# The MLP's first 512 channels by plain products in token halves, and GpSimd's sums moved to VectorE

## The chip, the cores and the metric

The kernel runs on one core of one Trainium2 chip. The metric is the device time of one execution in microseconds (us). Names of engines in the profile: PE is TensorE (PEld its weight loads), DVE is VectorE, ACT is ScalarE, POOL is GpSimd, SP is SyncE, whose queue issues the DMAs.

## The reference

One decoder block on 512 tokens of 1024 channels, float32, with two token mixers (a gated MLP over positions and a state-space scan) whose sum goes through an output projection, and then a channel MLP with 4096 hidden channels. The change is in the MLP:

```python
x = x + merged @ w_out
h2 = rms_norm(x, norm_mlp_g)
x = x + jnp.square(jax.nn.relu(h2 @ w_mlp_up)) @ w_mlp_down
return rms_norm(x, norm_final_g)
```

## The kernel before

Every float32 operand of a product is split into a high part (a ScalarE cast to the matmul's reduced float32 type) and a low part (a VectorE subtraction, "remainder" below), and every product is three matmuls: high by low, low by high, high by high (`mm3`, `trio`). Weights come in slabs of 128 x 1024, 512 KB each, on SP's queue; `parts_of` (L114 to L120) makes the pair `whi`, `wlo`, of which there are four buffers each. `Slabs.take` hands out the next pair and makes further ones ahead of time.

**The up-projection by seven products.** The 4096 hidden channels are eight blocks `u` of 512. For each block the transposed, normalised activations `h2` are four quadrants `b11`, `b12`, `b21`, `b22` (first index: half of the 1024 input channels; second: half of the 512 tokens), and the block's weights are four slabs. Instead of eight products of quadrants the kernel makes seven (the Strassen-Winograd form): it forms sums of weight slabs (`Up.sum`, L860 to L870) and sums of quadrants (`h2_sums`, L792), and seven products `(u, k)`, each of 8 trios, that is 24 matmuls of 256 columns (L155). The operand pairs made from `h2` are `hq[1]` to `hq[7]`. The products' results are put together with copies `kept` (L935), additions (L957), and `act` (L938 to L946: relu, square, cast on ScalarE, remainder on VectorE), which writes `aTs`, the down-projection's input.

**Order.** `items` (L886) is the order of the products and of the down-projection's slabs ("d"); four rounds `qd`, each of two blocks `u` and eight down slabs. In the first round, both blocks' products are interleaved (L883). The section is under a manual schedule: each engine keeps the order in which the program is written, so an instruction that waits holds up all that stands behind it on its engine.

**The start of the MLP.** The second half of the output projection runs token tile by token tile (`tok_major`, order "tokens"). After each of four tiles of 128 tokens `n2_evac` adds the residual, squares (ScalarE, with the sum), takes the power -1/2 (`rms_scale`, on GpSimd), applies the norm's gain (`gain`, two VectorE instructions of 128 x 512, L817), and `h2_tile` transposes the tile on TensorE and copies it into `h2` (L800, L801). `Weave` (`wv.at(delay, f)`) sets after how many matmul groups each step is issued; the delays are `H2D`. Tiles 0 and 1 are the first token half, tiles 2 and 3 the second. The first products use only the first token half (`hq[1]` is -b11, `hq[2]` is b21); tile 2 and tile 3 are transposed between these products. Then `h2_second` makes `hq[3]` and `hq[5]`, and three more quadrant sums follow ahead of products 3, 4 and 5 of the order (`H2AT`), two of them on GpSimd:

```python
h2_sums = (lambda: nc.vector.tensor_add(b12, b12, b22), lambda: nc.gpsimd.tensor_sub(b11, b11, b12),
           lambda: nc.gpsimd.tensor_sub(b21, b21, b12))
```

GpSimd also makes the remainder of `hq[3]` (L772) and one weight sum of block 0 (L870).

Of the kernel before, what the change touches and what calls it, by code (L numbers as in the profile page):

```python
# [11 lines left out]
F32 = mybir.dt.float32  # L12
F32R = mybir.dt.float32r
AF = mybir.ActivationFunctionType
ALU = mybir.AluOpType
# [3 lines left out]
P = 128  # L19
T = 512  # L20
# [11 lines left out]

SD, SA, SI, SS, SB, SC = 9, (12, 20), 8, 7, 9, 9


H2D = 0, 1.5, 2.5, 5.5, .4, 2.2, .6, 6, 7.9, 7.9
H2AT, NR = (3, 4, 5), 6
HPAD = 16, 32, 32, 32, 32, 32, 32, 48
WARM = 2, 0

# [10 lines left out]
def block_kernel(ctx: ExitStack, tc: tile.TileContext, x, w_v, w_all, w_up, wspt, pvec, hvec, g_mix, g_mlp, g_fin, v_g, v_b,  # L51
# [17 lines left out]
    def sm_tile():  # L69
        return ps.tile([P, T], F32, tag="sm", name="sm", bufs=4)  # L70


    class Slabs:
# [24 lines left out]
        def make(self):  # L98
            if self.todo:
                self.ready.append(self.todo.popleft()())  # L100
# [10 lines left out]
            self.ahead(ahead)  # L111
            return s

    def parts_of(raw):  # L114
        n = raw.shape[-1]
        hi = wpool.tile([P, SL], F32R, tag="whi", name="whi", bufs=4)[:, :n]
        lo = wpool.tile([P, SL], F32R, tag="wlo", name="wlo", bufs=4)[:, :n]
        nc.scalar.copy(hi, raw)  # L118
        nc.vector.tensor_sub(lo, raw, hi.bitcast(F32))  # L119
        return hi, lo  # L120
# [5 lines left out]
    class Weave:  # L126
# [3 lines left out]
        def at(self, delay, fn):  # L130
            heapq.heappush(self.due, (self.now + delay, self.seq, fn))
            self.seq += 1
# [25 lines left out]
    def cut(pair, *idx):  # L158
        return tuple(a[(slice(None),) + idx] for a in pair)

    def wk(w, k, n=P):
        return cut(w, slice(k * n, (k + 1) * n))
# [599 lines left out]
    n2.tile([P, HPAD[7]], F32, name="hq_pad8")  # L762
    b11, b12, b21, b22 = (h2[:, 4 * j:4 * j + 4, 256 * l:256 * l + 256] for j in range(2) for l in range(2))

    def hi_of(k, a, scale=1.0):
        if scale == 1.0:
            nc.scalar.copy(hq[k][0], a)
        else:
            nc.scalar.activation(hq[k][0], a, AF.Copy, scale=scale)

    def lo_of(k, a):
        (nc.gpsimd if k == 3 else nc.vector).tensor_sub(hq[k][1], a, hq[k][0].bitcast(F32))  # L772

    def h2_one():
        hi_of(1, b11, -1.0)
        nc.vector.scalar_tensor_tensor(hq[1][1], b11, -1.0, hq[1][0].bitcast(F32), ALU.mult, ALU.subtract)

    def h2_two():
        hi_of(2, b21)
        lo_of(2, b21)  # L780

    h2_first = h2_one, h2_two

    def h2_second():
        nc.vector.tensor_sub(b12, b11, b12)
        hi_of(3, b22)
        hi_of(5, b12)
        lo_of(3, b22)
        lo_of(5, b12)


    h2_sums = (lambda: nc.vector.tensor_add(b12, b12, b22), lambda: nc.gpsimd.tensor_sub(b11, b11, b12),  # L792
               lambda: nc.gpsimd.tensor_sub(b21, b21, b12))
    h2_ops = ((6, b12), (7, b11), (4, b21))

    def h2_tile(h, t):
        for b in range(2):
# [7 lines left out]
    def n2_evac(t, acc):  # L805
        res_evac(1)(t, acc)
        xt, h = x1[:, t, :], nr.tile([P, DM], F32, tag="rms_h", name="rms_h", bufs=1)
        ss = small.tile([P, 1], F32, tag="rms_ss", name="rms_ss", bufs=4)
        rs = []

        def square():
            nc.scalar.activation(hq[4][0].rearrange("p k t -> p (k t)"), xt, AF.Square, accum_out=ss)

        def gain():
            for b in range(2):
                hb = slice(b * T, (b + 1) * T)
                nc.vector.scalar_tensor_tensor(h[:, hb], xt[:, hb], rs[0], gbc[:, hb], ALU.mult, ALU.mult)  # L817

        def scale():
            rs.append(rms_scale(ss))  # L820

        steps[t] = square, scale, gain, lambda: h2_tile(h, t)
        for i in range(3 if t < 2 else 0):
            wv.at(H2D[i], steps[t][i])
        if t < 2:
            wv.at(H2D[3], steps[t][3])
        elif t == 2:
            wv.at(H2D[4], h2_one)
            wv.at(H2D[5], square)
        else:  # L830

            h2_two()
            square()
            for f in (steps[2][1], steps[2][2], scale):
                f()
            for d, f in zip(H2D[6:], (gain, steps[2][3], steps[3][3], h2_second)):
                wv.at(d, f)


# [3 lines left out]
    class Up:  # L843

        def __init__(self):
            self.free, self.n, self.at = list(tiles), 0, {}

            self.todo = [(u, i) for u in range(2 * NQ) for i in (2, 3, None, 0, 1)]
            j = self.todo.index((1, 2))
            self.todo[j:j + 5] = [(1, 0), (1, 1), (1, 2), (1, 3), (1, None)]  # L850

        def pump(self):
            while self.free and self.todo:
# [6 lines left out]
        def sum(self, u, n):  # L860
            self.pump()
            at = lambda i: self.at[u, i]
            if n == 1:
                nc.vector.tensor_add(at(None), at(2), at(3))  # L864
            elif n == 2:
                nc.vector.tensor_add(at(0), at(None), at(0))
            elif n == 3:
                nc.vector.tensor_add(at(2), at(2), at(0))
            else:
                (nc.vector if u else nc.gpsimd).tensor_add(at(1), at(0), at(1))  # L870

        def make(self, u, k):
            self.pump()
            i = {1: 0, 2: 1, 5: None, 6: 0, 3: 1, 7: 2, 4: 3}[k]
            r = parts_of(self.at[u, i])
            if k > 2:
                self.free.append(self.at.pop((u, i)))
                self.pump()
            return r

    up = Up()
    later = [(0, 1), (0, 2), (0, 5), (0, 6), (0, 3), (0, 7), (1, 1), (0, 4), (1, 2), (1, 5), (1, 6), (1, 3), (1, 7)]
    orders = [[(0, 1), (0, 2), (1, 1), (1, 2), (0, 5), (0, 6), (0, 3), (0, 7), (1, 5), (0, 4), (1, 6), (1, 3), (1, 7)]]  # L883
    orders += [later] * (NQ - 1)

    items = []  # L886
    for qd in range(NQ):
        items += [("p", 2 * qd + u, k) for u, k in orders[qd]] + [("d", qd, 0), ("p", 2 * qd + 1, 4)] + [("d", qd, i) for i in range(1, 8)]
    place = {it: j for j, it in enumerate(items)}

    sums_at = collections.defaultdict(list)
    for u in range(2, 2 * NQ):
        j = place["p", u, 5]
        for n, d in ((1, 7), (3, 6), (2, 4), (4, 2)) if u % 2 else ((1, 7), (3, 6), (2, 4), (4, 3)):
            sums_at[j - d].append((u, n))
    sums_at[1].append((0, 4))
    j = place["p", 1, 5]
    for n, d in ((1, 5), (3, 4), (2, 3), (4, 1)):
        sums_at[j - d].append((1, n))
    for it in items:  # L900
        slabs.todo.append(slabs.slab if it[0] == "d" else lambda it=it: up.make(*it[1:]))

    slabs.early = True
# [3 lines left out]
    def n2_evac_(t, acc):  # L907
        n2_evac(t, acc)
        if t == 0:
            up.sum(0, 1)  # L910
            up.sum(0, 3)
        if t == 1:
            up.sum(0, 2)

    up.pump()
    tok_major(mg_t, n2_evac_, order="tokens", ahead=3)
    slabs.ahead(3)
    mg_cm.__exit__(None, None, None)
    mp = ctx.enter_context(pool("mlp"))
    tiles.append(mp.tile([P, SL], F32, name="ut7"))  # L920
# [2 lines left out]
    nc.sync.dma_start(gfb, g_fin.partition_broadcast(P))  # L923
    banks = [acc_tile() for _ in range(4)]
    bank_a, bank_c, bank_d = (banks[0], banks[3]), banks[1], banks[2]
    kept = {}
    aTs = {}
    after, last = collections.defaultdict(list), collections.defaultdict(list)
# [9 lines left out]
    def act(j, u, i, l, src):  # L938

        r_ = mp.tile([P, 2, 256], F32, tag="relu", name="relu", bufs=2)  # L940
        nc.scalar.activation(r_, src.rearrange("p (c t) -> p c t", c=2), AF.Relu)
        nc.scalar.activation(r_, r_, AF.Square)
        n = 4 * (u % 2) + 2 * i
        hi, lo = cut(aTs[u // 2], slice(n, n + 2), slice(256 * l, 256 * l + 256))
        nc.scalar.copy(hi, r_)
        last[j + 1].append(lambda: nc.vector.tensor_sub(lo, r_, hi.bitcast(F32)))  # L946

    def evac(j, u, k, bank, i=0, l=0):

        if k in (1, 5, 6):  # L950
            keep(u, k, bank)
        elif k == 4:
            after[j].append(lambda: act(j, u, 1, 0, bank))
        else:
            k0, i, l = {2: (1, 0, 0), 3: (6, 0, 1), 7: (5, 1, 1)}[k]
            t = kept.pop((u, k0))
            nc.vector.tensor_sub(t, bank, t)  # L957

            jj = NR if j < NR else j
            after[jj].append(lambda: act(jj, u, i, l, t))  # L960

    sums = [[] for _ in range(NT)]

# [22 lines left out]
                nc.sync.dma_start(out[t * P:(t + 1) * P, c], o[:, c])  # L986
        return evac

    BANK = {2: lambda u: bank_c, 5: lambda u: bank_d, 3: lambda u: bank_d}
    accs = {}  # L990
    for j, it in enumerate(items[:-4]):

        if j and items[j - 1][0] == "p":
            _, u, k = items[j - 1]
            evac(j, u, k, BANK.get(k, lambda u: bank_a[u % 2])(u))
        if j == NR:
            nr_cm.__exit__(None, None, None)
            ap = ctx.enter_context(pool("act"))
            new_act(0)
        late = H2AT.index(j) if j in H2AT else None  # L1000
        if late is not None:
            h2_sums[late]()
        for u, n in sums_at.pop(j, ()):
            up.sum(u, n)
        for f in last.pop(j, ()):
            f()
        w = slabs.take(3)
        if late is not None:
            hi_of(*h2_ops[late])
        for f in after.pop(j, ()):  # L1010
            f()
        if late is not None:
            lo_of(*h2_ops[late])
        if it[0] == "p":
            _, u, k = it
            if k == 1 and u % 2 == 0 and u:
# [95 lines left out]
```

## Time and profile before

| | before |
|---|---|
| median of 3 runs | 1074.12 us (1073.47 to 1074.26) |
| the profiled execution's own time | 1073.14 us |
| its span, first to last instruction | 1071.4 us |
| TensorE busy | 1049.6 us, 98% |
| VectorE busy | 682.2 us, 64% |
| ScalarE busy | 505.6 us, 47% |
| GpSimd busy | 150.8 us, 14% |
| mean granted TensorE clock | 0.994 |

The times are the device's; the span leaves out what lies before the first and after the last instruction, 1.7 us here. Busy shares are means over the whole kernel, whose stages have different limits. Matmul records overlap, since a matmul is shown from its start to the end of its passage through the array; the pace is read from the distance of two starts.

### The profile page before, as it was taken

Reading aid. Unit: us, or ns where it says so; the run is one execution under the profiler, and the core shown is the slowest. Engines: PE = TensorE matmul, PEld = TensorE weight load, DVE = VectorE, ACT = ScalarE, POOL = GpSimd, SP = SyncE. Lnnn points to the kernel's source line nnn. Section 1 sums busy time; section 2 is a strip of 40 time slices with the busy share of each in tenths; the row PEclk is TensorE's granted clock in tenths of the full one; section 3 lists DMA queues with packets and bytes.
Section 4 is the critical chain, followed back from the end, with each engine's and each line's share of the span. In section 5 each row is a group of like instructions: output and inputs, shape, how many; then the busy total and the mean of one; then the engine's idle time right before and its main releaser. Section 6 shows DMA issues by size and latency. Waiting matters only on the chain. (4 is left out here: it accounts for less than half of the span.)

```text
span 1071.4 us, 14498 instructions
## 1 busy us (share of the span) xinstructions
PE 1049.6 (98%) x5685; PEld 910.2 (85%) x5685; DVE 682.2 (64%) x1087; ACT 505.6 (47%) x753; POOL 150.8 (14%) x192
## 2 busy tenths in 40 slices
PE   8999999999999999999999999996999999999997
PEld 7988888888888888888888888886989989988986
DVE  5572444446887995657778865369746746745743
ACT  4743333334546547444465532254824733723742
POOL 3020000001432342300324300014000000000000
PEclk9999999999999999999999999998999999999999
DMA  6433224232333233332323233721432432331032
GB/s 204 143 118 118 79 80 138 97 99 79 99 98 118 99 99 102 100 101 96 107 86 99 72 125 98 272 63 59 139 98 79 137 100 79 118 104 55 21 99 79
DMA packets 34630, 111.39 MB, mean 104 GB/s; under 512 B 3969, under 2 KB 4737, under 8 KB 34562
## 3 DMA queue, kind: packets, MB, share of 16 engines
q1 hardware_dynamic: 34560, 110.46, 32.5%
q8 instruction: 45, 0.74, 0.3%
q14 instruction: 23, 0.19, 0.0%
q10 hardware_dynamic: 2, 0.00, 0.0%
HBM read 108.29 MB, written 2.16 MB: 103 GB/s over the span
## 5 line engine op out<-in xcount | busy, mean ns | idle before, releaser
L119 DVE TENSOR_TENSOR wlo<-wraw,whi 128x1024 fp32r<-128x1024 f32 (+1 forms) x146 | 175.5, 1203 | 119.5 <-ACT whi L118 119.5
L118 ACT CAST whi<-wraw 128x1024 fp32r<-128x1024 f32 (+1 forms) x146 | 149.9, 1028 | 165.0 <-PE acc L149 75.9
L147 PE MATMUL acc<-hTl,whi 128*128 128x512 f32 x448 | 179.8, 401 | 0.0
L149 PE MATMUL acc<-hTh,whi 128*128 128x512 f32 x448 | 174.8, 390 | 0.0
L148 PE MATMUL acc<-hTh,wlo 128*128 128x512 f32 x448 | 174.6, 390 | 0.0
L119 DVE TENSOR_TENSOR wlo<-ut,whi 128x1024 fp32r<-128x1024 f32 x56 | 70.5, 1261 | 54.3 <-ACT whi L118 54.2
L149 PEld LDWEIGHTS acc<-hTh,whi 128*128 128x128 f32 x448 | 84.1, 188 | 18.1
L148 PEld LDWEIGHTS acc<-hTh,wlo 128*128 128x128 f32 x448 | 84.4, 188 | 15.0
L147 PEld LDWEIGHTS acc<-hTl,whi 128*128 128x128 f32 x448 | 84.4, 188 | 14.7
L118 ACT CAST whi<-ut 128x1024 fp32r<-128x1024 f32 x56 | 58.8, 1051 | 69.1 <-PE sm L149 52.7
L570 DVE SCALAR_TENSOR_TENSOR cv<-acc,pv,cv 128x511 f32<-128x511 f32 (+2 forms) x96 | 71.5, 745 | 29.3 <-ACT cv L568 28.6
L147 PE MATMUL sm<-wlo,ah 128*128 128x512 f32 (+1 forms) x232 | 89.5, 386 | 0.0
L149 PE MATMUL sm<-whi,ah 128*128 128x512 f32 (+1 forms) x232 | 89.4, 386 | 0.0
L148 PE MATMUL sm<-whi,al 128*128 128x512 f32 (+1 forms) x232 | 89.4, 385 | 0.0
L147 PE MATMUL acc<-wlo,hTh 128*128 128x512 f32 (+1 forms) x208 | 77.9, 375 | 0.2
L148 PE MATMUL acc<-whi,hTl 128*128 128x512 f32 (+1 forms) x208 | 75.6, 363 | 0.0
L149 PE MATMUL acc<-whi,hTh 128*128 128x512 f32 (+1 forms) x208 | 75.4, 364 | 0.0
L230 POOL TENSOR_TENSOR rms_rs<-rms_ms,mhalf 128x1 f32<-128x1 f32 x12 | 8.6, 721 | 428.7 <-DVE rms_ms L228 428.7
L149 PEld LDWEIGHTS sm<-whi,ah 128*128 128x128 f32 x232 | 43.6, 188 | 8.9
L148 PEld LDWEIGHTS sm<-whi,al 128*128 128x128 f32 x232 | 43.6, 188 | 8.5
L147 PEld LDWEIGHTS sm<-wlo,ah 128*128 128x128 f32 x232 | 43.6, 188 | 8.4
L147 PE MATMUL acc<-yBl,whi 128*128 128x512 f32 x128 | 50.6, 395 | 0.0
(268 smaller groups left out, 2364.9 us busy)
## 6 DMA issues: line engine op xcount, KB each, us to landing
wraw<-in_w_all SPq DMA_DIRECT2D x136, 512.0 KB, 3.5
ut<-in_w_up SPq DMA_DIRECT2D x32, 512.0 KB, 3.6
lm<-csd SPq DMA_DIRECT2D x32, 256.0 KB, 4.5
wraw<-in_w_v SPq DMA_DIRECT2D x10, 352.0 KB, 3.2
x<-in_x SPq DMA_DIRECT2D x4, 512.0 KB, 6.8
out<-ut SPq DMA_DIRECT2D x8, 256.0 KB, 2.0
xt<-in_x SPq DMA_DIRECT2D x3, 512.0 KB, 6.3
wraw<-in_w_v SPq DMA_DIRECT2D x4, 176.0 KB, 5.6
```

The lines of the kernel that those rows point to most:

```text
L118: nc.scalar.copy(hi, raw)
L119: nc.vector.tensor_sub(lo, raw, hi.bitcast(F32))
L147: nc.tensor.matmul(o, st[0], mv[1], start=first, stop=False)
L148: nc.tensor.matmul(o, st[1], mv[0], start=False, stop=False)
L149: nc.tensor.matmul(o, st[0], mv[0], start=False, stop=last)
L230: nc.gpsimd.tensor_tensor(rs, ms, mhalf, ALU.pow)
L570: nc.vector.scalar_tensor_tensor(cv[:, s_:], acc[:, :T - s_], cw[:, 3 - s_:4 - s_], cv[:, s_:], ALU.mult, ALU.add)
```

## The change

Block `u = 0` no longer goes by seven products. Its 512 channels are four channel blocks of 128, and each is computed plainly in two token halves: item ("c", 0) multiplies the first token half (`hq[1]` = b11, `hq[2]` = b21) by the four raw slabs, item ("c", 1) the second half (`hq[6]` = b12, `hq[3]` = b22) by the same four pairs, which stay in their buffers in between. Each half is 32 trios, 96 matmuls of 256 columns, into four banks `bank_0`. Between the two halves stand products 1 and 2 of block 1; its other products follow the second half. The four channel blocks are evacuated by `act0` (three ScalarE instructions and a remainder) from item `NR` = 4 on.

The quadrant sums are formed with other signs (T1 = b12 - b11, T2 = b22 - T1, T3 = T2 - b11, T4 = b21 - T2) and all on VectorE, T1 at item 1 and the others at item 2; so are all weight sums. GpSimd keeps only the powers of the norm. The operand pairs `hq[6]` and `hq[4]` that the later products need are made in the middle of the second half (`h2_end`). The pairs of block 1's first two weight slabs are made at the evacuation of token tile 0, into the space of `hq[7]` and `hq[4]` (`early`), and the square's scratch moves from `hq[4]` to `hq[5]`. Blocks 2 to 7 keep the seven-product form.

```diff
-H2D = 0, 1.5, 2.5, 5.5, .4, 2.2, .6, 6, 7.9, 7.9
-H2AT, NR = (3, 4, 5), 6
+H2D = 0, 1.5, 2.5, 5.5, .4, 2.2, .6, 6, 8.5, 8.5
+NR = 4
+
+HALVES, B12 = (0, 2, 1, 3), 6
...
+    def quad(k, a):
+        nc.scalar.copy(hq[k][0], a)
+        nc.vector.tensor_sub(hq[k][1], a, hq[k][0].bitcast(F32))
+
+    def h2_b12():
+        quad(B12, b12)
+        quad(3, b22)
+
+    def h2_t1():
+        nc.vector.tensor_sub(b12, b12, b11)
+        quad(5, b12)
+
+    def h2_t234():
+        nc.vector.tensor_sub(b22, b22, b12)
+        nc.vector.tensor_sub(b11, b22, b11)
+        nc.vector.tensor_sub(b21, b21, b22)
...
-            self.todo = [(u, i) for u in range(2 * NQ) for i in (2, 3, None, 0, 1)]
-            j = self.todo.index((1, 2))
-            self.todo[j:j + 5] = [(1, 0), (1, 1), (1, 2), (1, 3), (1, None)]
+            self.todo = [(0, i) for i in HALVES] + [(1, i) for i in (0, 1, 2, 3, None)]
+            self.todo += [(u, i) for u in range(2, 2 * NQ) for i in (2, 3, None, 0, 1)]
...
-                (nc.vector if u else nc.gpsimd).tensor_add(at(1), at(0), at(1))
+                nc.vector.tensor_sub(at(1), at(1), at(0))
...
+        if qd == 0:
+            items += [("c", 0)] + [("p", 1, k) for k in (1, 2)] + [("c", 1)] + [("p", 1, k) for k in (5, 6, 3, 7)]
+        else:
+            items += [("p", 2 * qd + u, k) for u, k in later]
+        items += [("d", qd, 0), ("p", 2 * qd + 1, 4)] + [("d", qd, i) for i in range(1, 8)]
...
+    for n, d in ((1, 1), (3, 1), (2, 2), (4, 2)):
+        sums_at[d].append((1, n))
+    slabs.todo.extend((lambda i=i: up.raw(i)) for i in HALVES)
+    for it in items[4:]:
...
         if t == 0:
-            up.sum(0, 1)
-            up.sum(0, 3)
-        if t == 1:
-            up.sum(0, 2)
-
+
+            for k, j in ((1, 7), (2, 4)):
+                early.append(up.make(1, k, [a.rearrange("p k t -> p (k t)") for a in hq[j]]))
...
-    slabs.ahead(3)
+    slabs.ahead(4)
+    slabs.ready += early
...
+    bank_0 = [bank_d, bank_a[0], sm_tile(), sm_tile()]
+
+    def h2_end():
+        slabs.ahead(2)
+        quad(B12, b22)
+        quad(4, b21)
...
+    def act0(j, n, bank):
+
+        r_ = mp.tile([P, T], F32, tag="relu", name="relu", bufs=2)
+        nc.scalar.activation(r_, bank, AF.Relu)
+        nc.scalar.activation(r_, r_, AF.Square)
+        hi, lo = cut(aTs[0], n)
+        nc.scalar.copy(hi, r_)
+        last[j + 1].append(lambda: nc.vector.tensor_sub(lo, r_, hi.bitcast(F32)))
...
+            for n in range(4):
+                after[j + (n + 1) // 2].append(lambda n=n, jj=j + (n + 1) // 2: act0(jj, n, bank_0[n]))
...
+        if it[0] == "c":
+            half = it[1]
+            if half == 0:
+                ws = [slabs.take(0) for _ in range(4)]
+            for jk in range(2):
+                mv = hq[((1, 2), (B12, 3))[half][jk]]
+                for n in range(4):
+                    for kt in range(4):
+                        trio(bank_0[n][:, 256 * half:256 * half + 256], wk(ws[2 * jk + n // 2], 4 * (n % 2) + kt),
+                             cut(mv, kt), half == jk == kt == 0, jk == 1 and kt == 3)
+                if half == 1:
+                    (h2_end, h2_end2)[jk]()
+            continue
+        if j == 1:
+            h2_t1()
+        elif j == 2:
+            h2_t234()
+            quad(7, b11)
```

## Rows read from the trace of the kernel before

**Rows 1.** The page's 40 slices: TensorE's busy tenths and its granted clock.
```profile
PE   8999999999999999999999999996999999999997
...
PEclk9999999999999999999999999998999999999999
```

**Rows 2.** Table by stretches: length, busy (instructions) PE, PEld, DVE, ACT, POOL; clock, DMA.
```profile
724.00:732.00 8.00, 5.27 (x31) 5.06 (x32) 6.81 (x5) 4.11 (x5) 4.24 (x2) 0.79 0.18 66
732.00:744.00 12.00, 6.32 (x53) 5.94 (x51) 12.00 (x8) 7.05 (x8) 6.78 (x3) 0.92 0.16 45
744.00:749.00 5.00, 5.00 (x24) 5.00 (x25) 5.00 (x6) 0.00 (x0) 0.00 (x0) 0.52 0.23 51
```

**Rows 3.** TensorE in order of time: start, duration, instruction, [idle before and its releaser].
```profile
716.82 0.28 PE L155 MATMUL acc<-hq1l,whi 128*128 128x256 f32 x1
...
721.06 1.03 PE L800 MATMUL sm<-ident,rms_h 128*128 128x128 f32 x8
721.85 0.37 PE L155 MATMUL acc<-hq2l,whi 128*128 128x256 f32 x1
...
726.64 1.38 PE L800 MATMUL sm<-ident,rms_h 128*128 128x128 f32 x8 [3.16 <-DVE rms_h L817]
...
734.00 0.36 PE L155 MATMUL acc<-hq2l,whi 128*128 128x256 f32 x1 [1.63 <-ACT whi L118]
...
743.95 0.58 PE L155 MATMUL acc<-hq6l,whi 128*128 128x256 f32 x1 [4.05 <-DVE hq6l L772]
...
763.00 0.28 PE L155 MATMUL acc<-hq3l,whi 128*128 128x256 f32 x1
...
765.83 0.28 PE L155 MATMUL acc<-hq7l,whi 128*128 128x256 f32 x1
...
768.53 0.28 PE L155 MATMUL acc<-hq7h,whi 128*128 128x256 f32 x1
```

**Rows 4.** VectorE in order of time, from the gain of tile 2 on.
```profile
719.57 1.42 DVE L817 SCALAR_TENSOR_TENSOR rms_h<-x,rms_rs,gbc 128x512 f32<-128x512 f32 x2 [0.66 <-POOL rms_rs L230]
...
720.97 2.35 DVE L119 TENSOR_TENSOR wlo<-ut,whi 128x1024 fp32r<-128x1024 f32 x2
723.76 3.48 DVE L817 SCALAR_TENSOR_TENSOR rms_h<-x,rms_rs,gbc 128x512 f32<-128x512 f32 x2 [0.44 <-POOL rms_rs L230]
...
740.53 3.36 DVE L772 TENSOR_TENSOR hq6l<-h,hq6h 128x1024 fp32r<-128x1024 f32 x1
```

**Rows 5.** GpSimd in order of time, same stretch.
```profile
721.13 2.60 POOL L230 TENSOR_TENSOR rms_rs<-rms_ms,mhalf 128x1 f32<-128x1 f32 x1 [1.59 <-DVE rms_ms L228]
723.70 2.33 POOL L870 TENSOR_TENSOR ut<-ut,ut 128x1024 f32<-128x1024 f32 x1
...
736.20 3.32 POOL L792 TENSOR_TENSOR h<-h 128x1024 f32<-128x1024 f32 x1 [4.03 <-DVE h L792]
739.49 3.32 POOL L793 TENSOR_TENSOR h<-h 128x1024 f32<-128x1024 f32 x1
```

**Rows 6.** The page's DMA issues: tile, queue, count, KB each, us to landing.
```profile
ut<-in_w_up SPq DMA_DIRECT2D x32, 512.0 KB, 3.6
```

**Rows 7.** ScalarE in order of time, from the last slabs of w_out on.
```profile
689.27 1.05 ACT L118 CAST whi<-wraw 128x1024 fp32r<-128x1024 f32 x1 [6.40 <-DMA wraw<-in_w_all]
...
697.56 1.05 ACT L118 CAST whi<-ut 128x1024 fp32r<-128x1024 f32 x1 [4.53 <-PE acc L149]
...
749.27 0.59 ACT L935 COPY kept<-acc 128x512 f32<-128x512 f32 x1 [5.38 <-PE acc L155]
749.75 1.05 ACT L118 CAST whi<-ut 128x1024 fp32r<-128x1024 f32 x1
750.70 0.63 ACT L941 ACTIVATE relu<-kept 128x512 f32<-128x512 f32 x1
...
752.56 0.63 ACT L941 ACTIVATE relu<-kept 128x512 f32<-128x512 f32 x1
...
762.39 0.59 ACT L941 ACTIVATE relu<-acc 128x512 f32<-128x512 f32 x1
...
764.20 0.58 ACT L935 COPY kept<-acc 128x512 f32<-128x512 f32 x1
```

More of the change, by code (lines that the diff above doesn't have):

```diff
@@ L112, in take, with parts_of @@
             return s
-    def parts_of(raw):
+    def parts_of(raw, pair=None):
         n = raw.shape[-1]
-        hi = wpool.tile([P, SL], F32R, tag="whi", name="whi", bufs=4)[:, :n]
-        lo = wpool.tile([P, SL], F32R, tag="wlo", name="wlo", bufs=4)[:, :n]
+        hi, lo = pair or (wpool.tile([P, SL], F32R, tag=n_, name=n_, bufs=4)[:, :n] for n_ in ("whi", "wlo"))
         nc.scalar.copy(hi, raw)
@@ L763, in block_kernel @@
     b11, b12, b21, b22 = (h2[:, 4 * j:4 * j + 4, 256 * l:256 * l + 256] for j in range(2) for l in range(2))
[L765 to L794, printed above, removed]
+    def quad(k, a):
[11 more added lines that the diff above has]
+        nc.vector.tensor_sub(b21, b21, b22)
     def h2_tile(h, t):
@@ L811, in square @@
         def square():
-            nc.scalar.activation(hq[4][0].rearrange("p k t -> p (k t)"), xt, AF.Square, accum_out=ss)
+            nc.scalar.activation(hq[5][0].rearrange("p k t -> p (k t)"), xt, AF.Square, accum_out=ss)
         def gain():
@@ L827, in n2_evac @@
         elif t == 2:
-            wv.at(H2D[4], h2_one)
+            wv.at(H2D[4], lambda: quad(1, b11))
             wv.at(H2D[5], square)
         else:
-            h2_two()
+            quad(2, b21)
             square()
@@ L835, in n2_evac @@
                 f()
-            for d, f in zip(H2D[6:], (gain, steps[2][3], steps[3][3], h2_second)):
+            for d, f in zip(H2D[6:], (gain, steps[2][3], steps[3][3], h2_b12)):
                 wv.at(d, f)
@@ L865, in sum, with make, raw, drop @@
             elif n == 2:
-                nc.vector.tensor_add(at(0), at(None), at(0))
+                nc.vector.tensor_sub(at(0), at(None), at(0))
             elif n == 3:
-                nc.vector.tensor_add(at(2), at(2), at(0))
+                nc.vector.tensor_sub(at(2), at(0), at(2))
             else:
-                (nc.vector if u else nc.gpsimd).tensor_add(at(1), at(0), at(1))
-        def make(self, u, k):
+                nc.vector.tensor_sub(at(1), at(1), at(0))
+        def make(self, u, k, pair=None):
             self.pump()
             i = {1: 0, 2: 1, 5: None, 6: 0, 3: 1, 7: 2, 4: 3}[k]
-            r = parts_of(self.at[u, i])
+            r = parts_of(self.at[u, i], pair)
             if k > 2:
-                self.free.append(self.at.pop((u, i)))
-                self.pump()
-            return r
+                self.drop(u, i)
+            return r
+        def raw(self, i):
+            self.pump()
+            r = parts_of(self.at[0, i])
+            self.drop(0, i)
+            return r
+        def drop(self, u, i):
+            self.free.append(self.at.pop((u, i)))
+            self.pump()
     up = Up()
     later = [(0, 1), (0, 2), (0, 5), (0, 6), (0, 3), (0, 7), (1, 1), (0, 4), (1, 2), (1, 5), (1, 6), (1, 3), (1, 7)]
-    orders = [[(0, 1), (0, 2), (1, 1), (1, 2), (0, 5), (0, 6), (0, 3), (0, 7), (1, 5), (0, 4), (1, 6), (1, 3), (1, 7)]]
-    orders += [later] * (NQ - 1)
     items = []
     for qd in range(NQ):
-        items += [("p", 2 * qd + u, k) for u, k in orders[qd]] + [("d", qd, 0), ("p", 2 * qd + 1, 4)] + [("d", qd, i) for i in range(1, 8)]
+        if qd == 0:
[3 more added lines that the diff above has]
+        items += [("d", qd, 0), ("p", 2 * qd + 1, 4)] + [("d", qd, i) for i in range(1, 8)]
     place = {it: j for j, it in enumerate(items)}
@@ L895, in block_kernel @@
             sums_at[j - d].append((u, n))
[L896 to L900, printed above, removed]
+    for n, d in ((1, 1), (3, 1), (2, 2), (4, 2)):
+        sums_at[d].append((1, n))
+    slabs.todo.extend((lambda i=i: up.raw(i)) for i in HALVES)
+    for it in items[4:]:
         slabs.todo.append(slabs.slab if it[0] == "d" else lambda it=it: up.make(*it[1:]))
@@ L909, in n2_evac_ @@
         if t == 0:
-            up.sum(0, 1)
-            up.sum(0, 3)
-        if t == 1:
-            up.sum(0, 2)
+            for k, j in ((1, 7), (2, 4)):
+                early.append(up.make(1, k, [a.rearrange("p k t -> p (k t)") for a in hq[j]]))
+    early = []
     up.pump()
     tok_major(mg_t, n2_evac_, order="tokens", ahead=3)
-    slabs.ahead(3)
+    slabs.ahead(4)
+    slabs.ready += early
     mg_cm.__exit__(None, None, None)
@@ L925, in block_kernel, with h2_end2 @@
     bank_a, bank_c, bank_d = (banks[0], banks[3]), banks[1], banks[2]
+    bank_0 = [bank_d, bank_a[0], sm_tile(), sm_tile()]
[3 more added lines that the diff above has]
+        quad(4, b21)
+    def h2_end2():
+        pass
     kept = {}
@@ L946, in act, with evac @@
         last[j + 1].append(lambda: nc.vector.tensor_sub(lo, r_, hi.bitcast(F32)))
-    def evac(j, u, k, bank, i=0, l=0):
+    def evac(j, u, k, bank):
         if k in (1, 5, 6):
@@ L956, in evac @@
             t = kept.pop((u, k0))
-            nc.vector.tensor_sub(t, bank, t)
-            jj = NR if j < NR else j
+            nc.vector.tensor_add(t, bank, t)
+            jj = max(j, NR)
             after[jj].append(lambda: act(jj, u, i, l, t))
+    def act0(j, n, bank):
[5 more added lines that the diff above has]
+        last[j + 1].append(lambda: nc.vector.tensor_sub(lo, r_, hi.bitcast(F32)))
     sums = [[] for _ in range(NT)]
@@ L987, in fin @@
         return evac
-    BANK = {2: lambda u: bank_c, 5: lambda u: bank_d, 3: lambda u: bank_d}
+    BANK = {2: lambda u: bank_c, 5: lambda u: bank_d if u > 1 else bank_c, 3: lambda u: bank_d if u > 1 else bank_c}
     accs = {}
@@ L996, in block_kernel @@
         if j == NR:
+            wv.flush()
             nr_cm.__exit__(None, None, None)
@@ L999, in block_kernel @@
             new_act(0)
-        late = H2AT.index(j) if j in H2AT else None
-        if late is not None:
-            h2_sums[late]()
+            for n in range(4):
+                after[j + (n + 1) // 2].append(lambda n=n, jj=j + (n + 1) // 2: act0(jj, n, bank_0[n]))
         for u, n in sums_at.pop(j, ()):
@@ L1006, in block_kernel @@
             f()
-        w = slabs.take(3)
-        if late is not None:
-            hi_of(*h2_ops[late])
+        if j < NR:
+            w = slabs.take(0) if j in (1, 2) else None
+        else:
+            w = slabs.take(3)
         for f in after.pop(j, ()):
             f()
-        if late is not None:
-            lo_of(*h2_ops[late])
+        if it[0] == "c":
[16 more added lines that the diff above has]
+            quad(7, b11)
         if it[0] == "p":
```

## The prediction, before the result

> **What bounds the kernel now.** I read the page first. TensorE is busy in nearly every slice, so only TensorE's idle time and its slow time can be won, and both sit in one place: the slices near two thirds of the span, where its digit falls to 6 and the clock's digits fall to 8 [rows 1]. The table by stretches then shows the stretch around the start of the MLP in numbers: TensorE idles in two of three stretches, and the granted clock is 0.79, 0.92 and 0.52 of full speed, that is, parts of it run at 1.2 instead of 2.4 GHz [rows 2]. After that stretch no wait of TensorE is listed up to the end of the kernel.
>
> TensorE's own order of time gives the places [rows 3]. The first up-product starts at 716.82 and the last product ahead of the first down-projection starts its last matmul at 768.53, so the stage is 768.65 - 716.82 = 51.83 us long. It holds 13 products. One product at full clock is 765.83 - 763.00 = 2.83 us for 24 matmuls of 256 columns, 0.118 us each, so 13 are 36.8 us. The 16 transposes of token tiles 2 and 3 take 721.85 - 721.06 = 0.79 us per eight, 1.6 us. The waits are 3.16 us ahead of tile 3's transposes (plus 0.3 us between its two halves), 1.63 us for a weight slab and 4.05 us for `hq6l`: 9.1 us. The remaining 4.3 us are the clock: after the first and after the third wait matmuls come at half pace; in the worst stretch 24 take 5.00 us [rows 2] where 2.83 would do.
>
> Why those waits are so long is seen on VectorE and GpSimd. `gain` of tile 2 takes 1.42 us for its two halves, `gain` of tile 3 takes 3.48 [rows 4], and during it GpSimd runs its weight sum of L870 from 723.70 to 726.03 [rows 5]. `hq6l` takes 3.36 us where a remainder pass of the same shape takes 2.35 / 2 = 1.18 [rows 4], and during it GpSimd runs L793, which follows L792's 3.32 us [rows 5]. So on the two engines together each pass lasts about three times VectorE's time alone.
>
> **The change part by part.** I list TensorE's work in the new order, and then ask of each operand whether it is there.
>
> *More matmuls.* The four channel blocks of `u = 0` as plain products are 64 trios, 192 matmuls, where seven products were 168: 24 more, +2.83 us [rows 3]. All of it lies on the path.
>
> *Up to the first product: nothing.* At the evacuation of token tile 0 two weight sums (L864, L868) leave VectorE and the remainder passes for (1, 1) and (1, 2) take their place: two passes of one shape against two; L866 at tile 1 goes without a substitute. Their two casts come ahead of tile 0's square on ScalarE, but ScalarE is then idle. `pump` loads a seventh weight tile early, ahead of the w_out slabs on SP's queue. At most this shifts them by one landing, 3.6 us [rows 6]. The slab that ScalarE waited for until 689.27 would be cast by 693.9, and its remainder and that of the slab behind it are done by 697; TensorE first wants it when it has left the first pass, shown by the cast that starts on TensorE's release at 697.56 [rows 7]. So it costs 0 (bounds 0 and 1). The sign changes (`quad(1, b11)` without scale -1, subtractions for additions) are the same passes.
>
> *Transposes of tile 3.* `gain(3)` still starts at about 723.76: before it VectorE has two remainder passes (now of raw slabs 1 and 3), and the power on GpSimd that takes 2.60 us beside them [rows 4, 5]; both stay. But L870's sum is gone from GpSimd, so `gain(3)` should take 1.42, with halves ready at 724.5 and 725.2. TensorE gets there after 17 trios and tile 2's transposes: 716.82 + 17 x 0.354 + 0.79 = 723.6, waits 0.9 us, and 0.3 more for the second half; it resumes at 725.7 (before 727.8, on a clock that soon fell). I take 1.1 us for both waits.
>
> *Rest of the first half and pair (1, 1), (1, 2).* 15 trios end at 731.0, and two products on `hq1` and `hq2` end at 736.7. Their weights were split at tile 0 into the space of `hq7` and `hq4`. The wait of 1.63 us for a slab is gone with it.
>
> *Second half.* It wants `hq6` (now b12) at 736.7 and `hq3` (b22) 16 trios later. After the transposes ScalarE copies two halves (726.5), casts each, and VectorE's remainders follow: about 728.8 and 729.9. 8 us to spare, where before b12, b22 and T2 were wanted one after another.
>
> *Sums on VectorE.* From 729.9 VectorE has in its queue: four sums of weights, T1, `hq5l`, T2 to T4, `hq7l`, one `kept` addition, remainders of (1, 5) and (1, 6), `hq6l` and `hq4l`. With 1.14 to 1.2 us for a large pass and two waits for casts that ends at 747.7. The remainders of (1, 5) end at 744.3, wanted at 748.0 when the second half's 32 trios (11.3 us) are over; (1, 6) 745.5, wanted at 750.8; `hq5` 735.7, `hq7` 742.6. No wait, smallest margin 3.7 us. What was at 3.3 us on GpSimd costs 1.2 and lies under TensorE's plain products; without that cover each pass would cost its 1.2.
>
> *A new wait on ScalarE.* Behind the plain products ScalarE is late. The cast of (1, 7) waits for the slab buffer that the second half holds until 748.3. Behind it in program order stand the act of product 2, `act0(0)`, the copy `kept` of (1, 5), the cast of the down slab, `act0(1)`, `act0(2)`, and only then `kept` of (1, 6), which frees the bank that product (1, 7) adds to. A cast takes 750.70 - 749.75 = 0.95 of the queue, an act from `kept` 752.56 - 750.70 = 1.86, an act from a bank 764.20 - 762.39 = 1.81, a copy 749.75 - 749.27 = 0.48 [rows 7], and the last copy is counted to its end: 748.3 + 0.95 + 1.86 + 1.81 + 0.48 + 0.95 + 2 x 1.81 + 0.58 = 758.6. TensorE is through (1, 5), (1, 6), (1, 3) at 748.0 + 3 x 2.83 = 756.5. So it waits 2.1 us, for `kept` of (1, 6). The earlier copy, of (1, 5), is done at 753.5, when (1, 3) is due at 753.7: just no wait. Bounds for this term: 0, if the order of buffers leaves ScalarE free earlier, and 3.
>
> *The clock.* TensorE fell to 1.2 GHz after the waits of 3.16 and 4.05 us, but the products after the wait of 1.63 us ran at full speed [rows 2, 3]. The new waits of 0.9 and 2.1 us are nearer to 1.63, so I charge nothing. If it falls after the 2.1, one product of 24 at half pace costs 5.0 - 2.8 = 2.2 us, and for the range I allow the same after the first wait. [...]
>
> **The sum.** New stage: 14 x 2.83 = 39.6, transposes 1.6, waits 1.1 + 2.1, and 0.3 for restarts: 44.7 us against 51.8. The first down-projection starts at 761.5 instead of 768.65, and what it needs (`act0(0)` and `act0(1)`, done by 757, and the slab) is there; `act0(3)` is done by 762.1, before the slab that reads it. From there the program is the same and TensorE never waits, so nothing is given back. The profiled execution took 1073.14 us (span 1071.40 and 1.7 around it), and becomes 1066.0; the median of the runs shown is 0.98 above it: 1074.12 - 7.1 = **1067.0 us**.
>
> **Rivals.**
> *Slow clock after the new waits.* All as above, but the clock falls after one of the two. For it: it fell twice here. Against it: not after 1.63 us. +2.2: 1069.2 us. Chance 0.20.
> *No ScalarE wait.* The copy of (1, 6) comes in time. For it: which buffer a cast waits for is decided by the allocator. Against: four buffers, and all are in use. 1064.9 us. Chance 0.12.
> *GpSimd was not what stretched `gain(3)` and the waits stay.* The change then does not remove what it seems to: 3.46 us of wait ahead of tile 3 and 1.4 of slow clock come back, +3.8: 1070.8. For it: nothing but that one coincidence is shown per case; against: two cases, both about threefold. Chance 0.08. Other waits in the new order that I priced at zero would end in the same place, 1070 to 1073; 0.06.
> *Slower than before.* The slow clock holds on: a matmul at 1.2 GHz takes 0.208 instead of 0.118 us, so 7.1 + 2.1 = 9.2 us are eaten once some 100 matmuls, four of the stage's fourteen products, run slow. The place is the products after the two new waits. For it: 24 ran slow in one go. Against: after both falls the clock was back within some 24 matmuls. All 192 slow would give 1067.0 + 17.3 = 1084. Chance 0.05, and 0.03 for a time within 0.2% of before.
>
> **How the numbers follow.** The likeliest case has 0.46 and gives 1067.0, by itself 1065.9 to 1068.1. With both ends of the unknown costs (no wait at all but the transposes': 1064.5; slow clock twice: 1071.4) the range is 1063.8 to 1071.2; it leaves out the slower case, the one near no change and part of the third. 0.2% of this kernel, 2.1 us, is about what a measurement can tell from no change. Cases that are faster by more: 0.46 + 0.20 + 0.12 + 0.08 + 0.05 = 0.91; within it 0.04; slower 0.05.
>
> **What would show it.** In the profile after: `gain(3)` at 1.4 us; tile 3's transposes at about 724.5; no GpSimd work after the last power; the second half's 96 matmuls back to back from 736.7; one wait of some 2 us ahead of product (1, 7), put down to `kept`; the first down matmul near 761.5; no granted clock under 0.9 in any of these stretches. I am wrong if the clock falls in the plain products, if the w_out slabs come late, or if waits show up in the down-projection.

## The result and the profile after

The changed kernel takes 1067.18 us (median of 4 runs, 1065.44 to 1067.94) against 1074.03 of the kernel before; the ratio is 0.9935, 95% interval 0.9917 to 0.9952. The prediction said 1067.0 us. The profiled execution took 1067.94 us with a span of 1066.2.

The page of the kernel after, TensorE's busy tenths and granted clock in 40 slices (before: [rows 1]):

```profile
PE   9999999999999999999999999999999999999997
...
PEclk9999999999999999999999999999999999999999
```

The slices that fell to 6 and 8 are full now. TensorE's order of time, with the starts of the first product, of tile 3's transposes, of product (1, 7) and of the first down-projection (before: [rows 3]):

```profile
719.19 0.28 PE L155 MATMUL acc<-hq1l,whi 128*128 128x256 f32 x1
...
726.49 1.29 PE L786 MATMUL sm<-ident,rms_h 128*128 128x128 f32 x8 [0.26 <-DVE rms_h L803]
...
760.48 0.38 PE L155 MATMUL acc<-hq7l,whi 128*128 128x256 f32 x1 [1.96 <-ACT kept L943]
...
763.41 0.39 PE L147 MATMUL sm<-wlo,ah 128*128 128x512 f32 x1
```

And all waits of TensorE on other engines from there to the end, total, times, longest:

```profile
PE acc L155 <- ACT kept L943: 2.0, 1, 2.0
PE sm L786 <- DVE rms_h L803: 0.7, 2, 0.4
```

The stage lasts 763.41 - 719.19 = 44.22 us where it lasted 51.83: 7.6 us less, with 24 matmuls more. The waits of 3.16, 1.63 and 4.05 us are gone, and two are left: tile 3's, of 0.26 and 0.4 for its two halves, and one of 1.96 us ahead of product (1, 7). The table by stretches shows the second half's 96 matmuls without a gap, the wait, and no slow clock (columns as in [rows 2]):

```profile
737.00:748.00 11.00, 11.00 (x96) 11.00 (x95) 10.93 (x11) 5.48 (x6) 0.00 (x0) 1.00 0.07 9
...
757.00:762.00 5.00, 3.04 (x26) 2.84 (x25) 2.55 (x4) 4.87 (x9) 0.00 (x0) 1.00 0.32 105
```

On VectorE the gain of tile 3 is back at 1.41 us, and GpSimd's last work up to the norm at the kernel's end is the power in front of it (before: [rows 4, 5]). VectorE, then GpSimd:

```profile
725.60 1.41 DVE L803 SCALAR_TENSOR_TENSOR rms_h<-x,rms_rs,gbc 128x512 f32<-128x512 f32 x2
```
```profile
723.49 1.46 POOL L230 TENSOR_TENSOR rms_rs<-rms_ms,mhalf 128x1 f32<-128x1 f32 x1 [1.59 <-DVE rms_ms L228]
```

ScalarE shows the new wait as it was forecast: the cast of (1, 7) starts when the second half has left its buffer, and `kept` of (1, 6) follows 9.7 us later:

```profile
750.17 1.05 ACT L118 CAST whi<-ut 128x1024 fp32r<-128x1024 f32 x1 [1.75 <-PE sm L155]
...
759.85 0.58 ACT L943 COPY kept<-acc 128x512 f32<-128x512 f32 x1
```

**2.4 us that are not the change's.** The MLP starts at 719.19 in this execution, at 716.82 in the profiled one of before. Some 2 us of it are there after 63 us already (the evacuations of v's last pass start at 63.1 instead of 61.0), and up to the output projection's second half both kernels issue the same instructions in the same order. ScalarE waits longer for the weight slabs of v, longest for the one shown, and TensorE then twice for ScalarE. ScalarE and TensorE in order of time, after:

```profile
44.93 0.78 ACT L118 CAST whi<-wraw 128x704 fp32r<-128x704 f32 x1 [2.96 <-DMA wraw<-in_w_v]
```
```profile
47.54 0.43 PE L147 MATMUL acc<-wlo,hTh 128*128 128x352 f32 x1 [0.64 <-ACT v L503]
...
51.78 0.43 PE L147 MATMUL acc<-wlo,hTh 128*128 128x352 f32 x1 [0.76 <-ACT v L503]
```

So the profiled executions differ by 1073.14 - 1067.94 = 5.2 us: 7.6 won in the stage, 2.4 lost to late loads at the start of this one execution.

### The profile page after: what moved, and what is told of

Its sections match the earlier page's. It is cut to its first block, busy times and chain, and to the rows that moved or that the text cites. A ratio compares the mean times of both kernels' runs of the same rounds, so it can differ in the third digit from the quotient of the medians.

```text
span 1066.2 us, 14522 instructions
## 1 busy us (share of the span) xinstructions
PE 1049.7 (98%) x5709; PEld 909.8 (85%) x5709; DVE 671.0 (63%) x1082; ACT 501.8 (47%) x748; POOL 138.4 (13%) x188
## 4 chain that ended last, share of the span: by engine, by line
PE 73%; DVE 13%; ACT 4%; DMA 4%; POOL 4%; issue 3%; SPq 0%; POOLq 0%; ACTq 0%; DVEq 0%
PE acc L147 14%; PE acc L149 14%; PE acc L148 14%; PE acc L155 12%; PE sm L147 5%; PE sm L149 5%; PE sm L148 5%; DVE cv L570 3%; DVE wlo L119 2%; DMA wraw<-in_w_v 2%; DVE lm L610 1%; POOL xD L668 1%; PE sm L664 1%; POOL lm L613 1%; POOL yrs L677 1%
## 5 line engine op out<-in xcount | busy, mean ns | idle before, releaser
L119 DVE TENSOR_TENSOR wlo<-ut,whi 128x1024 fp32r<-128x1024 f32 x51 | 62.2, 1222 | 53.4 <-ACT whi L118 53.4
L118 ACT CAST whi<-ut 128x1024 fp32r<-128x1024 f32 x51 | 53.5, 1051 | 70.9 <-PE sm L149 52.8
```

## The experiments

Theory A: GpSimd's passes made the waits, since each lasts long and stretches what VectorE does beside it; the plain products give cover for the rest; what is left is ScalarE's late copy, and the clock where it follows a wait. The rivals: one of the two parts does it all; the copy's wait only moves when it is mended.

**The changed kernel again.** No edit.

> The changed kernel once more, unaltered. The first 45 us hold the same instructions in the same order in both kernels, so the 2.4 us by which the profiled execution after was late at the start of the MLP should be a matter of that execution: the MLP should start at 716.5 to 719.5 us and end its stage (first product to first down matmul) 44.2 us later in any case. Theory A (the stage alone is changed): a median of 1065 to 1068 us and a stage of 44.0 to 44.5. Rival (the change itself delays the start): the MLP starts at 719 or later again.

Median 1067.35 us, ratio 0.9934 (0.9919 to 0.9948). The MLP starts at 717.02, so the late start was that one execution's. But the stage did not keep to 44.2 us, it took 762.52 - 717.02 = 45.50: behind the wait, now 2.05 us, the clock fell to 1.2 GHz. TensorE in order of time: the pace of product (1, 7) goes from 0.118 to 0.213 us per matmul within it:

```profile
717.02 0.28 PE L155 MATMUL acc<-hq1l,whi 128*128 128x256 f32 x1
...
758.32 0.38 PE L155 MATMUL acc<-hq7l,whi 128*128 128x256 f32 x1 [2.05 <-ACT kept L943]
...
759.25 0.28 PE L155 MATMUL acc<-hq7h,wlo 128*128 128x256 f32 x1
759.37 0.28 PE L155 MATMUL acc<-hq7h,whi 128*128 128x256 f32 x1
...
760.81 0.41 PE L155 MATMUL acc<-hq7h,wlo 128*128 128x256 f32 x1
761.02 0.41 PE L155 MATMUL acc<-hq7h,whi 128*128 128x256 f32 x1
...
762.52 0.63 PE L147 MATMUL sm<-wlo,ah 128*128 128x512 f32 x1
```

By stretches, columns length, PE busy (instructions), clock, DMA:

```profile
755.00:760.00 5.00, 2.95 (x25) 0.97 0.35 105
760.00:765.00 5.00, 5.00 (x23) 0.69 0.18 25
```

In the eight executions of this kernel the mean granted clock is 0.999 three times, at 1064.92, 1065.44 and 1067.94 us (the last with the late start), 0.997 four times, at 1067.29 to 1067.55, and 0.998 once, at 1066.81. So the same wait lets the clock fall in some executions, by the mean clock four or five of these eight, and not in others. By these times the fall costs about 2 us; in the trace of this run product (1, 7) takes 762.52 - 758.32 = 4.20 us instead of the 763.41 - 760.48 = 2.93 of the first trace after.

**The sums alone.** The kernel before with GpSimd's four passes on VectorE:

```diff
-        (nc.gpsimd if k == 3 else nc.vector).tensor_sub(hq[k][1], a, hq[k][0].bitcast(F32))
+        nc.vector.tensor_sub(hq[k][1], a, hq[k][0].bitcast(F32))
...
-    h2_sums = (lambda: nc.vector.tensor_add(b12, b12, b22), lambda: nc.gpsimd.tensor_sub(b11, b11, b12),
-               lambda: nc.gpsimd.tensor_sub(b21, b21, b12))
+    h2_sums = (lambda: nc.vector.tensor_add(b12, b12, b22), lambda: nc.vector.tensor_sub(b11, b11, b12),
+               lambda: nc.vector.tensor_sub(b21, b21, b12))
...
-                (nc.vector if u else nc.gpsimd).tensor_add(at(1), at(0), at(1))
+                nc.vector.tensor_add(at(1), at(0), at(1))
```

> The kernel before with one part of the change: GpSimd's remainder of hq3, its two quadrant sums and its weight sum go to VectorE; the seven products of block 0 stay. Theory A (GpSimd's passes made the waits, by lasting three times as long and stretching VectorE's): the gain of tile 3 takes 1.42 us, hq6l 1.2 us, the waits ahead of tile 3 and of hq6 shrink from 3.2 and 4.1 us to about 1 and 0 to 1, the clock stays up, and with 24 matmuls fewer than the changed kernel the time is 1063.5 to 1067 us. Theory B (the cover of the plain products is what removes the waits, and VectorE with four more passes is late for hq6l): waits of 2 us or more stay ahead of hq6 and the time is 1069 to 1073 us.

1068.62 us, ratio 0.9954 (0.9938 to 0.9971): between the two theories' ranges. Gain and `hq6l` take 1.40 and 1.22 us, as theory A has it, but a wait of 2.88 us came ahead of product (1, 2), and the clock fell behind it. VectorE, then TensorE in order of time, the stretch (columns as in the run before), and TensorE's waits ahead of products:

```profile
723.47 1.40 DVE L817 SCALAR_TENSOR_TENSOR rms_h<-x,rms_rs,gbc 128x512 f32<-128x512 f32 x2
...
730.53 0.68 DVE L957 TENSOR_TENSOR kept<-acc,kept 128x512 f32<-128x512 f32 x1
...
735.67 1.22 DVE L772 TENSOR_TENSOR hq6l<-h,hq6h 128x1024 fp32r<-128x1024 f32 x1
```
```profile
731.36 0.55 PE L155 MATMUL acc<-hq2l,whi 128*128 128x256 f32 x1 [2.88 <-DVE kept L957]
```
```profile
730.00:735.00 5.00, 3.64 (x18) 0.66 0.02 7
```
```profile
PE acc L155 <- DVE kept L957: 4.4, 3, 2.9
...
PE acc L155 <- ACT kept L935: 0.5, 1, 0.5
```

(1, 2) waits for its bank, which the addition of (0, 2) reads, and that addition stands behind the quadrants' passes in VectorE's queue. VectorE is busy without a gap over 28 us here, which neither kernel was, with 26.81 us before and 24.17 after (columns as in [rows 2]; first this run, then the kernel after):

```profile
724.00:752.00 28.00, 23.20 (x176) 22.20 (x176) 28.00 (x29) 18.84 (x25) 0.00 (x0) 0.94 0.24 75
```
```profile
724.00:752.00 28.00, 27.70 (x235) 27.32 (x234) 24.17 (x23) 13.38 (x17) 0.95 (x1) 1.00 0.30 95
```

Tile 3's first wait is 0.55 us, 0.26 in the changed kernel, with the power at 1.46 us in both: the change also moves these transposes back by one trio (`H2D`), which is 0.35 us of work.

**The sums alone, with another bank for (1, 2).** This tells whether that bank or VectorE's full queue is the limit.

```diff
-    BANK = {2: lambda u: bank_c, 5: lambda u: bank_d, 3: lambda u: bank_d}
+    BANK = {2: lambda u: bank_d if u == 1 else bank_c, 5: lambda u: bank_d if u else bank_c, 3: lambda u: bank_d if u else bank_c}
```

> The kernel before with GpSimd's sums on VectorE, and product (1, 2) in another bank (block 0's products 5 and 3 change places with it), so that it doesn't wait for the addition of (0, 2) in VectorE's queue, which cost 2.9 us and a fall of the clock in the run with the sums alone. Theory A (VectorE's queue, full without a gap there, is the limit, and the plain products are what relieves it): the wait comes back ahead of hq6 or of the next bank, 2 to 3 us, and the time stays at 1066 to 1068.5 us, above the changed kernel with its wait mended. Rival (that bank was all that kept the seven products behind): waits under 1 us in all from there, and 1062.5 to 1064.5 us.

1068.56 us, ratio 0.9958 (0.9945 to 0.997), the same as without it. (This run and the two of `act0` below are from a second chip, where the kernel before takes 1073.45 us; on the first it takes 1073.31.) A wait came back ahead of `hq6`, and VectorE is again busy for 28.00 of 28 us. TensorE's waits ahead of products:

```profile
PE acc L155 <- DVE hq6l L772: 2.5, 1, 2.5
PE acc L155 <- DVE kept L957: 1.8, 1, 1.8
...
PE acc L155 <- ACT kept L935: 0.4, 1, 0.4
```

These waits add up to 4.7 us, 4.9 without the other bank: they moved and stayed as long. So VectorE's queue is the limit, and the plain products relieve it: block 0 needs no weight sums then, and no quadrant sums.

**The plain products alone.** The changed kernel with T3, T4, the remainder of `hq[3]` and one weight sum back on GpSimd:

```diff
-        nc.vector.tensor_sub(b11, b22, b11)
-        nc.vector.tensor_sub(b21, b21, b22)
+        nc.gpsimd.tensor_sub(b11, b22, b11)
+        nc.gpsimd.tensor_sub(b21, b21, b22)
...
-        nc.vector.tensor_sub(hq[k][1], a, hq[k][0].bitcast(F32))
+        (nc.gpsimd if k == 3 else nc.vector).tensor_sub(hq[k][1], a, hq[k][0].bitcast(F32))
...
-                nc.vector.tensor_sub(at(1), at(1), at(0))
+                (nc.gpsimd if u == 1 else nc.vector).tensor_sub(at(1), at(1), at(0))
```

This does not put everything back as it was: block 0 has no weight sums any more, so the one on GpSimd is now of block 1 and runs later, not beside the gain of tile 3.

> The changed kernel with the other part undone: T3, T4, the remainder of hq3 and one weight sum go back to GpSimd; the plain products stay. Theory A (GpSimd's passes are the cost wherever they are): T3 and T4 take 3.3 us each, VectorE's passes beside them two to three times their time, the remainders of (1, 5) and (1, 6) come too late and TensorE waits 2 to 4 us more ahead of products 5 to 7: 1069 to 1072 us. Theory B (the cover suffices for either engine): within 0.7 us of the changed kernel.

1068.84 us, ratio 0.995 (0.9935 to 0.9965). That is 1.5 us above the changed kernel on the same chip: the time is just under theory A's range and above theory B's. GpSimd's weight sum takes 3.31 us, T3 and T4 take 2.4 each, not 3.3. TensorE loses only 0.5 us to a late remainder and 0.5 to tile 3, not theory A's 2 to 4; the rest of the 1.5 is not placed. GpSimd in order of time, TensorE's waits, and its row and stretch around the wait ahead of (1, 7), behind which the clock fell here too:

```profile
738.10 3.31 POOL L855 TENSOR_TENSOR ut<-ut,ut 128x1024 f32<-128x1024 f32 x1 [7.03 <-DVE ut L851]
741.38 2.39 POOL L779 TENSOR_TENSOR h<-h 128x1024 f32<-128x1024 f32 x1
743.74 2.40 POOL L780 TENSOR_TENSOR h<-h 128x1024 f32<-128x1024 f32 x1
```
```profile
PE acc L155 <- ACT kept L943: 2.0, 1, 2.0
PE sm L786 <- DVE rms_h L803: 1.2, 2, 0.8
PE acc L155 <- DVE wlo L119: 0.5, 1, 0.5
```
```profile
759.81 0.39 PE L155 MATMUL acc<-hq7l,whi 128*128 128x256 f32 x1 [1.97 <-ACT kept L943]
```
```profile
760.00:765.00 5.00, 5.00 (x28) 0.66 0.08 32
```

So on this chip each part alone wins 4.5 to 4.7 of the 6.0 us that both win (before: 1073.31): the two gains do not add up, since each part by itself removes the waits of 3.16 and 4.05 us.

**GpSimd beside the gain.** The changed kernel with one weight sum of block 1 on GpSimd, behind the power of tile 3:

```diff
             for f in (steps[2][1], steps[2][2], scale):
                 f()
+            up.sum(1, 1, nc.gpsimd)
...
-    for n, d in ((1, 1), (3, 1), (2, 2), (4, 2)):
+    for n, d in ((3, 1), (2, 2), (4, 2)):
```

> The changed kernel with one weight sum of block 1 (the first, 128 x 1024) on GpSimd right behind the power of tile 3, so that it runs beside the gain of tile 3; VectorE has that sum less. Theory A: the gain of tile 3 takes 3 us or more as before the change, TensorE waits 2.5 to 3.3 us ahead of tile 3's transposes instead of 0.3, and the clock may fall behind it: 1069 to 1071.5 us. Rival (the stretch had another cause): the gain stays at 1.4 us and the time at 1067.

1068.63 us, ratio 0.995 (0.9935 to 0.9965). The gain's halves go from 0.74 to at most 2.84 us (minimum, median, maximum in ns), beside GpSimd's sum; TensorE waits 2.36 us ahead of tile 3, and later 1.96 us ahead of (1, 7), with the clock up behind it (last two rows):

```profile
L803 DVE SCALAR_TENSOR_TENSOR rms_h<-x,rms_rs,gbc x8: 739/748/2842, 705.3 to 725.7; 128x512 f32<-128x512 f32 x8
```
```profile
722.27 2.97 POOL L850 TENSOR_TENSOR ut<-ut,ut 128x1024 f32<-128x1024 f32 x1
```
```profile
725.93 1.29 PE L786 MATMUL sm<-ident,rms_h 128*128 128x128 f32 x8 [2.36 <-DVE rms_h L803]
...
759.93 0.39 PE L155 MATMUL acc<-hq7l,whi 128*128 128x256 f32 x1 [1.96 <-ACT kept L944]
```
```profile
760.00:765.00 5.00, 5.00 (x34) 1.00 0.03 11
```

This is the main cause of before's 3.16 us, made by itself. A part of the rest is the power in front of the gain, 2.60 us there and 1.46 here. The Trainium skill, "GPSIMD Engine Reference", section "8. Key points", says that GpSimd shares its SBUF interfaces with VectorE and that VectorE's instructions with two SBUF inputs meet it there; this run agrees, 2.84 us against 0.74 for one instruction. The clock stayed up (mean 0.999) in this execution. The median is 1.3 us above the changed kernel's on this chip, under the range I gave; but of the changed kernel's four executions here, the clock fell in three, by their mean clock. Mean clocks of 0.999 go with 1067.4 and 1068.4 us here, and, without a late start, with 1064.9 and 1065.4 in the changed kernel: 2 to 3.5 us more, for a wait that is 2.1 longer.

**`act0` spread.** One `act0` for each of items 4 to 7:

```diff
-                after[j + (n + 1) // 2].append(lambda n=n, jj=j + (n + 1) // 2: act0(jj, n, bank_0[n]))
+                after[j + n].append(lambda n=n, jj=j + n: act0(jj, n, bank_0[n]))
```

> The changed kernel with one act0 for each of items 4 to 7 instead of one, two and one for items 4, 5 and 6, so that the copy of (1, 6) has one act0 less (1.81 us) ahead of it on ScalarE. Theory A (ScalarE's order makes the wait of 2.0 us, and that wait is what lets the clock fall in some executions and not in others): the wait ahead of (1, 7) is 0.4 us or less, the clock stays up in every execution, mean clock 0.999, and the times lie close together at 1063 to 1064.5 us. Rival (the wait only moves on, to the banks that the down-projection takes over from act0): the gain is under 1 us, 1065 to 1067 us.

1064.02 us (1062.92 to 1064.52), ratio 0.9913 (0.9899 to 0.9928): the fastest version. The wait ahead of (1, 7) shrinks to 0.15 us, nothing takes its place, and the mean clock is 0.998 or 0.999 in all four executions (theory A said 0.999; the profiled one has 0.998 with full speed from 700 to 775 us, and 0.87 from 1050 us on, so a mean of 0.998 doesn't tell that the clock fell in this stage). TensorE in order of time, and its waits from there to the end:

```profile
757.07 0.39 PE L155 MATMUL acc<-hq7l,whi 128*128 128x256 f32 x1 [0.15 <-ACT kept L943]
```
```profile
PE acc L155 <- ACT kept L943: 0.2, 1, 0.2
```

**`act0` bunched.** The last three at item 5, so that the wait grows by one `act0`:

```diff
-                after[j + (n + 1) // 2].append(lambda n=n, jj=j + (n + 1) // 2: act0(jj, n, bank_0[n]))
+                after[j + (n > 0)].append(lambda n=n, jj=j + (n > 0): act0(jj, n, bank_0[n]))
```

> The changed kernel with the last three act0 all at item 5, ahead of the copy of (1, 6): the wait ahead of (1, 7) grows by 1.81 us to 3.8 us. Theory A (a longer wait lets the clock fall each time): the clock falls in every execution, mean clock 0.997 or lower, and the time is 1068.5 to 1070 us. Rival (whether the clock falls has nothing to do with the length of this wait): mean clocks of 0.999 appear among the executions, at 1066.5 to 1067 us.

1069.64 us (1068.01 to 1071.34), ratio 0.9966 (0.9956 to 0.9976). The wait is 3.8 us, and in all nine executions the mean clock is 0.996 or 0.997. TensorE by stretches:

```profile
755.00:760.00 5.00, 2.34 (x20) 0.97 0.30 109
760.00:765.00 5.00, 3.90 (x18) 0.50 0.01 3
765.00:770.00 5.00, 5.00 (x24) 0.85 0.28 107
```

From spread to bunched the wait grows by 3.6 us and the time by 5.6. The 2.0 us between are the clock's: in the profiles the 24 matmuls of (1, 7) take 766.39 - 761.10 = 5.29 us bunched and 760.01 - 757.07 = 2.94 spread, 2.35 us more.

## Why the prediction was right, and where it was not

- **GpSimd stretched the gain and `hq6l`**: right. For the gain it is shown by making it anew (0.74 us for one half without, 2.84 with a GpSimd pass beside it); for `hq6l` by taking GpSimd's passes away (3.36 us, then 1.22).
- **24 matmuls more on the path**: right; the stage holds 14 products' worth at the full pace.
- **Tile 3's transposes**: waits of 1.1 us forecast, 0.7 measured, since the power ahead of the gain took 1.46 instead of 2.60 us. In the plain products alone and with `act0` bunched it took 2.59, and the waits were 1.2.
- **The second half, VectorE's list, the seventh early load cost nothing**: right; no other wait of TensorE is listed.
- **ScalarE's copy of (1, 6)**: 2.1 us forecast, 1.96 and 2.05 measured, and mending it removed it.
- **"The clock: I charge nothing"**: this step failed. The nearest row, the wait of 1.63 us, did not carry over: behind the wait of 2 us the clock fell in four or five of eight executions by their mean clock, for about 2 us. I gave this rival 0.20.
- **The size**: the two executions with the clock up and no late start are at 1064.9 and 1065.4 us, below the forecast, and those in which it fell at 1067.3 to 1067.6. The median met 1067.0 by luck: the clock's fall, and in one execution the late loads, stood in for 1.6 to 2.1 us that my sum had too much: 0.5 in the stage's length, 1.0 from adding the distance between the profiled execution and the median, and a remainder that is not accounted for.
- **The range**: its lower end, 1063.8, lies 0.7 us under the 1064.5 that the prediction gives for no wait but the transposes', and no term of the sum stands for that.
- **One reading was wrong without consequence**: the wait of 1.63 us in [rows 3] is put down to a slab's cast; it was the bank of product (0, 2), whose addition on VectorE ended just ahead of it, at 733.86. The run with the sums alone names that addition for the same product. VectorE before, in order of time:

```profile
733.18 0.68 DVE L957 TENSOR_TENSOR kept<-acc,kept 128x512 f32<-128x512 f32 x1
```

What stays open: why a wait of 1.97 us (the plain products alone) or 2.05 (the repeated run) lets the clock fall, and one of 1.96 (the first run after, GpSimd beside the gain), or of 2.36 ahead of tile 3, does not. Near 2 us the length alone does not decide it, and nothing that was run shows what does.

## What to carry to other kernels

Where a stretch hangs on a chain of element-wise passes, count what runs on GpSimd beside VectorE as a cost to both, and look first for work for TensorE that needs none of the chain: 24 more matmuls (2.8 us) left the kernel 1.3 us faster than the sums alone, and 4.5 us once the late copy was mended. Then write down each engine's queue in program order with the durations of the profile; that found the one long wait left, 2.1 us against 1.96 to 2.05 measured, before the kernel ran. Moving three instructions past a copy was worth another 3 us: the wait, and the clock's fall behind it where it came. A wait of TensorE of about 2 us should be priced with a chance of a fall of the clock, here about 2 us on top in half of the executions; behind the longer waits shown here, of 2.5 to 4.1 us, the profiles show it each time.

## What the runs showed of the hardware

- The power of 128 numbers on GpSimd takes 0.55 us by itself and, beside two remainder passes on VectorE, 1.46 us in some executions and 2.6 in others of almost the same program; in the changed kernel and its variants the wait ahead of tile 3's transposes is 0.26 us with the first and 0.8 with the second.
- The clock: in the profiled executions it fell behind waits of TensorE of 1.97, 2.05, 2.52, 2.88, 3.16, 3.77 and 4.05 us, and stayed up behind 1.63, 1.83, 1.96 (twice) and 2.36. The other executions have only a mean clock: 0.996 or 0.997 in all 13 of the two kernels with 2.88 and 3.77 us, and 0.997 or 0.998 in five of the eight with 2.0. In the run bunched, the matmuls after the wait of 3.8 us ran at 1.2 GHz at once (0.50 over 5 us); in the repeated run, behind 2.05 us, the product began at 2.4 GHz and fell after ten matmuls.
- Loads in the first 50 us can land 2 us later in one execution than in another, with the same instructions up to there, and the rest of the kernel shifts by about that much.
